# A two-layer diffusion backbone on one core: modulation in two half passes on VectorE, merges in PSUM, eight plain units at the start of each FFN

## The chip, the cores and the metric

One core of a Trainium2 chip. The metric is the device time of one execution in microseconds; of several runs the median counts.

## What is computed

Two layers over 640 tokens (128 context, 512 latent) of width 1024. Each layer, cut to what matters here:

```python
mod = silu(cond) @ w_mod + b_mod                  # 6 x 1024 per condition (context, latent)
sh1, sc1, g1, sh2, sc2, g2 = split(mod, 6)
h = rms_norm(x, norm1) * (1 + sc1) + sh1
u_f, q_g, k_g, v_g, r_g, a_g, q_d, k_d, v_d, gates = split(h @ w_in)
y_f = fourier_mix(u_f) @ w_fou
y_g = (rms_norm(gated_linear_attention(...)) * silu(r_g)) @ w_gla_o
y_d = rms_norm(differential_attention(...)) @ w_diff_o
gf, gg, gd = split(sigmoid(gates), 3)
merged = gf * y_f + gg * y_g + gd * y_d
x = x + g1 * (merged @ w_out)
h2 = rms_norm(x, norm2) * (1 + sc2) + sh2
x = x + g2 * ((silu(h2 @ w_ff_gate) * (h2 @ w_ff_up)) @ w_ff_down)
```

Outputs are x, and each layer's attention keys, values and linear-attention states of the context tokens.

## The kernel before

**Layout.** Activations lie channels by tokens: eight tiles of 128 x 640, worked on in two halves of 320 columns (`SPLIT`). A weight unit is 128 x 1024 floats, loaded as two 128 x 512 tiles by SP, and split into a high and a low part (`split_weight`, lines 436 to 460): ScalarE casts the high part (line 450), GpSimd subtracts to get the low one (line 454). A product is three matmuls, high x high, high x low, low x high (`acc3`, line 492). `group` accumulates one half's product of eight (or, in `merge`, four) blocks in a buffer `main` of PSUM, of which there are two; `misc` and `big` have two each.

**Order.** TensorE's order is the program's. In the mixer the other engines are ordered by the framework's scheduler, in which earlier instructions of the program go first when they are ready; around the output projection and the FFN their order is the program's too (`manual_schedule`). Every engine works its queue in order. After each group `slot(cols)` is called. It advances the side work of the mixer (`queue`: the Fourier mixing, the linear attention, the preparation of queries and keys, the attention), and counts columns towards `rate`: each time `rate` columns have gone by, the generator `self.back` makes one step. While the linear attention's levels run, `hold` sets the count to zero. `finish_back` makes all steps that are left, at once.

**Modulation.** The 48 tiles of `mod` (128 channels each, two conditions) come in two ways.
- On TensorE: `mod_load` brings 32 tiles of `w_mod`, `mod_first` multiplies them with the conditions (line 734), ScalarE copies the rows (line 740), a transpose and VectorE's adds (line 746) give `mod`. This serves tiles 0 to 15: of layer one at the start of the kernel, and of layer two through `mod_later` as `back` in layer one's FFN, at a rate of 1600 columns.
- On VectorE: `mod_next` loads the condition in four pieces (two conditions, two halves of the 1024 rows), applies silu, then loads the transposed weights (two halves of a tile) and sums products along the row (line 781), two instructions for a half of a tile. It runs for layer one's tiles 16 to 35 from the start of its mixer (rate 160) and 36 to 47 from the last branch's gates on (128); for layer two's 16 to 31 as `fill` between layer one's down-projections, and 32 to 47 from the gates of its last branch on (256).

**Branches.** A mixer projects and folds the Fourier input, then the linear attention's inputs, then those of the differential attention, one half of the heads at a time, with the Fourier branch's gates and merges between them and the linear-attention branch's after them; then the gates and the merges of the last branch, then the output projection. `merge` (line 1419) multiplies a branch by its output weights: ScalarE copies the product from PSUM to a tile `y` (line 1426), VectorE multiplies by the gate (lines 1428, 1430) and adds (line 1431); in the last branch the sum is split at once (lines 485, 486).

**FFN.** Four quarters of gate and up pairs, each followed by its down-projection. The first `AHEAD` = 6 weight units (three pairs) are plain: `first_four` begins four of them while the normalization is still under way (line 518), and `ffn_start` goes through the evictions (`gate`, lines 292 and 293; `up`, 297 and 298; `low`, 302), with `combine` (lines 859 to 885) between them, which forms the sums of activation blocks that the other pairs need. The other pairs are done in seven products of half the size each in place of eight (`gated`, line 562); their weights need sums, which VectorE forms in PSUM (lines 422 to 436) and splits (line 454). `last_sums` (line 887) splits four tiles more.

The lines that the change and the prediction's steps touch:

Of the kernel before, what the change touches and what calls it, by code (L numbers as in the profile page):

```python
# [12 lines left out]
F32 = mybir.dt.float32  # L13
# [4 lines left out]
ALU = mybir.AluOpType  # L18
# [241 lines left out]
def layout(i):  # L260
# [8 lines left out]
        "w_mod": np.concatenate([pack_mod(i["w_mod"][l]) for l in range(DEPTH)]),  # L269
        "w_modt": np.concatenate([pack_modt(i["w_mod"][l])[32:] for l in range(DEPTH)]),  # L270
# [34 lines left out]
class Kernel:  # L305
# [400 lines left out]
    def mod_load(self, c, l=0, ks=range(KT)):  # L706
        raws = []
        for k in ks:
            raws.append(self.unit("rawm")[:, :512])
            self.nc.sync.dma_start(raws[-1], self.a["w_mod"][(l * 4 + c) * KT + k])  # L710
        return raws

    def mod_later(self, l, small, mod, scale1):

        for c in range(4):
            raws = []
            first = self.mod_first(raws, c, small, mod, scale1)
            for ks in (range(4), range(4, KT)):
                raws += self.mod_load(c, l, ks)
                yield  # L720
                for _ in ks:
                    next(first, None)
                yield
            for _ in first:
                pass
# [26 lines left out]
    def mod_next(self, l, m0, m1, small, mod):  # L752

        nc = self.nc
        cond = {}
        for i in range(2):
            for k in range(2):
                cond[i, k] = self.unit("cond")[:, :512]
                nc.sync.dma_start(cond[i, k], self.a["cond_b"][:, i, k * 512 : (k + 1) * 512])
        yield  # L760
        ends = collections.deque()
        for i, k in [(i, k) for i in range(2) for k in range(2)] + [(None, None)]:
            if i is not None:
                ends.append(self.silu(cond[i, k], self.unit("cond_t")[:, :512]))
            if i is None or len(ends) > 1:
                ends.popleft()()
            yield
        todo = [(m, k) for m in range(m0, m1) for k in range(2)]
        raws = collections.deque()
        for n in range(len(todo) + 2):  # L770
            if n < len(todo):
                m, k = todo[n]
                raws.append(self.unit("rawm")[:, :512])
                nc.sync.dma_start(raws[-1], self.a["w_modt"][l * 64 + m * 2 + k - 32])
            if n >= 2:
                m, k = todo[n - 2]
                raw = raws.popleft()
                if k == 0:
                    sums = self.sm([P, 2, 2], "modsum", 3)
                for i in range(2):  # L780
                    nc.vector.scalar_tensor_tensor(  # L781
                        self.sm([P, 512], "junk", 1, mybir.dt.bfloat16), raw, 1.0, cond[i, k], op0=ALU.mult, op1=ALU.mult, accum_out=sums[:, i, k : k + 1]
                    )
                if k:
                    nc.vector.scalar_tensor_tensor(mod[:, m], sums[:, :, 0], small[:, S_BM + m : S_BM + m + 1], sums[:, :, 1], op0=ALU.add, op1=ALU.add)
            yield

# [692 lines left out]
    def mixer(self, l, h, small, backs, norms):  # L1480
        nc = self.nc

        if backs[0] is not None:
            self.back, self.rate = backs[0], 160
# [386 lines left out]
```

## Time and profile before

| | us |
|---|---|
| median of three runs | 2354.91 (2353.22 to 2359.13) |
| the profiled execution | 2363.46 |
| its span, first to last instruction | 2361.7 |
| TensorE busy | 2232.1 |
| VectorE busy | 1645.7 |
| ScalarE busy | 995.8 |
| GpSimd busy | 935.5 |

The profile names engines PE (TensorE; PEld its weight loads), DVE (VectorE), ACT (ScalarE), POOL (GpSimd) and SP (DMA issue). A stretch is a piece of the span. [...]

### The profile page before, as it was taken

Reading aid. Unit: us, or ns where it says so; the run is one execution under the profiler, and the core shown is the slowest. Engines: PE = TensorE matmul, PEld = TensorE weight load, DVE = VectorE, ACT = ScalarE, POOL = GpSimd, SP = SyncE. Lnnn points to the kernel's source line nnn. Section 1 sums busy time; section 2 is a strip of 40 time slices with the busy share of each in tenths; the row PEclk is TensorE's granted clock in tenths of the full one; section 3 lists DMA queues with packets and bytes.
Section 4 is the critical chain, followed back from the end, with each engine's and each line's share of the span. In section 5 each row is a group of like instructions: output and inputs, shape, how many; then the busy total and the mean of one; then the engine's idle time right before and its main releaser. Section 6 shows DMA issues by size and latency. Waiting matters only on the chain. (4 is left out here: it accounts for less than half of the span.)

```text
span 2361.7 us, 44422 instructions
## 1 busy us (share of the span) xinstructions
PE 2232.1 (95%) x16882; PEld 2183.9 (92%) x16882; DVE 1645.7 (70%) x3410; ACT 995.8 (42%) x2194; POOL 935.5 (40%) x771
## 2 busy tenths in 40 slices
PE   6989899999999899998989999999998998999999
PEld 4978899999899899998989999999998888999999
DVE  5797887685955857778764757857758667575674
ACT  3444446454234424241434554464633254242332
POOL 1342444352333634342433443535333255252433
PEclk9999999999999899999999999999999999999999
DMA  7443221112622272736242222212134322424433
GB/s 271 159 135 98 78 74 55 63 55 83 212 88 78 84 246 87 266 119 212 87 149 72 79 78 72 70 50 65 53 116 166 132 88 74 160 98 160 135 103 125
DMA packets 151382, 271.40 MB, mean 115 GB/s; under 512 B 19200, under 2 KB 31360, under 8 KB 151168
## 3 DMA queue, kind: packets, MB, share of 16 engines
q1 hardware_dynamic: 125824, 219.75, 28.6%
q10 hardware_dynamic: 25344, 48.80, 5.9%
q8 instruction: 133, 2.18, 0.4%
q14 instruction: 81, 0.66, 0.1%
HBM read 235.98 MB, written 27.79 MB: 112 GB/s over the span
## 5 line engine op out<-in xcount | busy, mean ns | idle before, releaser
L454 POOL TENSOR_TENSOR wl<-raw,wh 128x512 fp32r<-128x512 f32 x514 | 710.3, 1396 | 1105.6 <-ACT wh L450 956.9
L450 ACT CAST wh<-raw 128x512 fp32r<-128x512 f32 x518 | 314.8, 619 | 293.8 <-PE main L492 155.7
L492 PE MATMUL main<-hh,wh 128*128 128x320 f32 x936 | 294.8, 315 | 0.1
L492 PE MATMUL main<-hh,wl 128*128 128x320 f32 x936 | 289.6, 309 | 0.0
L492 PE MATMUL main<-hl,wh 128*128 128x320 f32 x936 | 289.5, 309 | 0.0
L781 DVE SCALAR_TENSOR_TENSOR junk<-rawm,cond 128x512 bf16<-128x512 f32 x256 | 225.5, 881 | 30.8 <-DMA rawm<-in_w_modt_dram 25.8
L492 PE MATMUL main<-wh,hh 128*128 128x256 f32 x800 | 234.6, 293 | 10.5 <-DVE rx L1472 5.3
L492 PE MATMUL main<-wl,hh 128*128 128x256 f32 x800 | 228.7, 286 | 0.0
L492 PE MATMUL main<-wh,hl 128*128 128x256 f32 x800 | 228.5, 286 | 0.0
L492 PE MATMUL main<-ah,wh 128*128 128x320 f32 x704 | 219.8, 312 | 6.9 <-DVE x L1453 5.6
L1453 DVE SCALAR_TENSOR_TENSOR x<-main,g,x 128x128 f32<-128x128 f32 (+2 forms) x240 | 97.3, 436 | 184.5 <-PE main L492 170.1
L492 PE MATMUL main<-ah,wl 128*128 128x320 f32 x704 | 217.5, 309 | 0.0
L492 PE MATMUL main<-al,wh 128*128 128x320 f32 x704 | 217.5, 309 | 0.0
L450 ACT CAST wh<-big 128x512 fp32r<-128x512 f32 x152 | 89.2, 587 | 261.4 <-DVE big L433 88.4
L492 PEld LDWEIGHTS main<-hh,wh 128*128 128x128 f32 x936 | 176.4, 189 | 0.9 <-DVE aT L1526 0.3
L492 PE MATMUL main<-h2h,wh 128*128 128x320 f32 x520 | 165.1, 318 | 12.4 <-DVE tt L297 6.4
L492 PEld LDWEIGHTS main<-hl,wh 128*128 128x128 f32 x936 | 176.3, 188 | 0.1
L492 PEld LDWEIGHTS main<-hh,wl 128*128 128x128 f32 x936 | 176.0, 188 | 0.0
L492 PEld LDWEIGHTS main<-wh,hh 128*128 128x128 f32 x800 | 155.9, 195 | 13.6 <-ACT tm L644 6.0
L492 PE MATMUL main<-h2l,wh 128*128 128x320 f32 x520 | 164.2, 316 | 0.0
L492 PE MATMUL main<-h2h,wl 128*128 128x320 f32 x520 | 164.0, 315 | 0.0
L492 PEld LDWEIGHTS main<-wl,hh 128*128 128x128 f32 x800 | 155.9, 195 | 0.0
(359 smaller groups left out, 6118.2 us busy)
## 6 DMA issues: line engine op xcount, KB each, us to landing
raw<-in_w_dram SPq DMA_DIRECT2D x556, 256.0 KB, 2.9
rawm<-in_w_modt_dram SPq DMA_DIRECT2D x128, 256.0 KB, 4.4
x<-xd ACTq DMA_DIRECT2D x64, 320.0 KB, 4.5
rawm<-in_w_mod_dram SPq DMA_DIRECT2D x64, 256.0 KB, 5.3
xd<-x ACTq DMA_DIRECT2D x48, 320.0 KB, 4.0
xd<-x ACTq DMA_DIRECT2D x48, 160.0 KB, 1.9
cond<-in_cond_b_dram SPq DMA_DIRECT2D x16, 256.0 KB, 4.6
x<-in_x_t_dram SPq DMA_DIRECT2D x12, 320.0 KB, 5.4
```

The source lines that it names most:

```text
L450: nc.scalar.copy(h, raw)
L454: (nc.vector if late or sums else nc.gpsimd).tensor_sub(lo, raw, h.bitcast(F32))
L492: mm = lambda w, x, first=False, last=False: nc.tensor.matmul(ps, w, x, start=first and not more, stop=last, skip_group_check=more)
L781: nc.vector.scalar_tensor_tensor(self.sm([P, 512], "junk", 1, mybir.dt.bfloat16), raw, 1.0, cond[i, k], op0=ALU.mult, op1=ALU.mult, accum_ ...
L1453: nc.vector.scalar_tensor_tensor(x[:, r], ps[:, r.start - s.start : r.stop - s.start], g[:, m, i : i + 1], x[:, r], op0=ALU.mult, op1=ALU.add)
```

## The change

- **Modulation.** `mod_later` and the part of `w_mod` for layer two go. `mod_next` makes two passes, one for each half of the 1024 rows, with two pieces of the condition each; the first pass leaves its sums in `mod`, the second adds its own and the bias. A weight tile is loaded one step ahead in place of two. Layer two's tiles 0 to 15 are the `fill` of layer one's FFN; each layer's tiles 16 to 47 run in its own mixer, from its start, at one step per 400 columns, and per 560 from the differential attention's inputs on, up to the `finish_back` at the mixer's end. `scale1` is then made by `mod_scale`, when the last tile of layer one's FFN is done.
- **Merge.** No copy to `y`: VectorE multiplies out of PSUM (first branch), or within it, and adds from there.
- **FFN.** `AHEAD` is 8: four pairs are plain in each layer. `up` of the fourth unit and the weights that follow the third go before `combine`'s second step; `low` comes one eviction later; `last_sums` is made in two parts, behind the first and the second product.
- `UNITS`, the number of 128 x 640 tiles in SBUF, is 59 in place of 58.

```diff
-UNITS = 58
-AHEAD = 6
+UNITS = 59
+AHEAD = 8
+MODT = (-32, 64)
+RATES = (400, 560)
...
     def mod_next(self, l, m0, m1, small, mod):
+        nc = self.nc
+        for k in range(2):
+            cond = [self.unit("cond")[:, :512] for _ in range(2)]
+            for i in range(2):
+                nc.sync.dma_start(cond[i], self.a["cond_b"][:, i, k * 512 : (k + 1) * 512])
             yield
+            end = self.silu(cond[0], self.unit("cond_t")[:, :512])
+            yield
+            end()
+            end = self.silu(cond[1], self.unit("cond_t")[:, :512])
+            yield
+            end()
+            raw = None
+            for m in range(m0, m1 + 1):
+                last, raw = raw, None
+                if m < m1:
+                    raw = self.unit("rawm")[:, :512]
+                    nc.sync.dma_start(raw, self.a["w_modt"][MODT[l] + 2 * m + k])
+                if last is not None:
+                    sums = mod[:, m - 1] if k == 0 else self.sm([P, 2], "modsum", 3)
+                    for i in range(2):
+                        nc.vector.scalar_tensor_tensor(
+                            self.sm([P, 512], "junk", 1, mybir.dt.bfloat16), last, 1.0, cond[i], op0=ALU.mult, op1=ALU.mult, accum_out=sums[:, i : i + 1]
+                        )
+                    if k:
+                        b = small[:, S_BM + m - 1 : S_BM + m]
+                        nc.vector.scalar_tensor_tensor(mod[:, m - 1], sums, b, mod[:, m - 1], op0=ALU.add, op1=ALU.add)
+                yield
...
-    def last_sums(self, xs, act):
-        for k in range(4):
+    def last_sums(self, xs, act, ks):
+        for k in ks:
             self.split(xs[k][:, SPLIT[1]], *act["T3"][k])
...
             ps = self.group(self.weight(l, u), (m % 2) * 4, 4, act, s)
-            y = self.unit("y")[:, s]
-            nc.scalar.copy(y, ps)
             if first:
-                nc.vector.scalar_tensor_tensor(merged[m][:, s], tg[:, s], 1.0, y, op0=ALU.add, op1=ALU.mult)
+                nc.vector.scalar_tensor_tensor(merged[m][:, s], tg[:, s], 1.0, ps, op0=ALU.add, op1=ALU.mult)
             else:
-                nc.vector.scalar_tensor_tensor(tg[:, s], tg[:, s], 1.0, y, op0=ALU.add, op1=ALU.mult)
-                nc.vector.tensor_add(merged[m][:, s], merged[m][:, s], tg[:, s])
+                nc.vector.scalar_tensor_tensor(ps, tg[:, s], 1.0, ps, op0=ALU.add, op1=ALU.mult)
+                nc.vector.tensor_add(merged[m][:, s], ps, merged[m][:, s])
...
+        self.back, self.rate = back, RATES[0]
...
         dact = []
+        self.rate = RATES[1]
         for pr in range(2):
...
-        self.finish_back()
-        self.back, self.rate = backs[1], 128 if l == 0 else 256
         tg = [self.gate(l, U_BR[2] + m, h) for m in range(KT)]
...
         self.group_to(last, self.weight(l, us[3]), h2, SPLIT[1])
+        acts[1].up(last, 1)
+        self.used(l, us[2])
         next(combine)
         acts[0].low(1)
-        acts[1].up(last, 1)
-        self.used(l, us[2])
         for i in range(4, AHEAD):
             for p in range(2):
                 ps = self.group(self.weight(l, us[i]), 0, KT, h2, SPLIT[p])
                 if i % 2 == 0:
                     acts[i // 2].gate(ps, p)
-                    next(combine, None)
                 else:
                     acts[i // 2].up(ps, p)
-                if i == 4:
-                    acts[1].low(1) if p == 0 else self.used(l, us[3])
-                elif p:
-                    self.used(l, us[4])
-                    self.used(l, us[5])
-        for p in range(2):
-            acts[2].low(p)
+                if p:
+                    self.used(l, us[3 if i == 4 else i])
+                    if i == 5:
+                        self.used(l, us[4])
+                next(combine, None)
+                if i % 2 or p == 0:
+                    acts[(i - 1) // 2].low(p if i % 2 else 1)
...
-                self.last_sums(x2, sums)
-                if back is not None:
-                    self.back, self.rate = back, 1600
+                for i in range(2):
+                    self.after(i + 1, lambda i=i: self.last_sums(x2, sums, range(2 * i, 2 * i + 2)))
...
-            mg, x2 = self.mixer(l, h, small, (None, later_mod(32, 48)) if l else (later_mod(16, 36), later_mod(36, 48)), norms)
+            mg, x2 = self.mixer(l, h, small, self.mod_next(l, 16, 48, small, mod), norms)
...
+                    scales.append(self.mod_scale(n_mod, n_small, S_N1, 8, "scale1"))
...
-                    l, h2, x2, combine, sums, first, g2, done, self.mod_later(l + 1, n_small, n_mod, scale1), self.mod_next(l + 1, 16, 32, n_small, n_mod)
+                self.ffn(l, h2, x2, combine, sums, first, g2, done, self.mod_next(l + 1, 0, 16, n_small, n_mod))
```

## Rows read from the trace of the kernel before

**Rows 1.** The page: the span; part 1 for TensorE (busy us, share, instructions)

```profile
span 2361.7 us, 44422 instructions
...
PE 2232.1 (95%) x16882; PEld 2183.9 (92%) x16882; DVE 1645.7 (70%) x3410; ACT 995.8 (42%) x2194; POOL 935.5 (40%) x771
```

**Rows 2.** Stretches: length, busy us (count) of PE, PEld, DVE, ACT, POOL; clock, DMA

```profile
71.40:304.60 233.20, 209.37 (x2085) 202.13 (x2083) 195.25 (x410) 103.12 (x224) 85.49 (x65) 0.96 0.36 114
1256.00:1465.30 209.30, 203.04 (x2084) 196.99 (x2083) 125.68 (x227) 103.95 (x224) 79.16 (x65) 0.99 0.26 77
304.60:632.90 328.30, 323.45 (x2357) 321.61 (x2356) 245.37 (x585) 160.37 (x403) 136.65 (x126) 1.00 0.27 87
1465.30:1793.60 328.30, 323.46 (x2357) 321.62 (x2356) 233.18 (x552) 160.37 (x403) 136.56 (x126) 1.00 0.24 77
632.90:672.10 39.20, 32.36 (x194) 30.78 (x193) 32.43 (x64) 16.05 (x38) 11.40 (x9) 0.91 0.31 101
1793.60:1835.90 42.30, 31.39 (x194) 29.73 (x193) 36.71 (x82) 15.86 (x37) 12.47 (x9) 0.96 0.46 156
672.10:733.20 61.10, 58.46 (x396) 57.65 (x395) 26.54 (x62) 19.30 (x43) 18.18 (x15) 1.00 0.31 100
1835.90:1902.30 66.40, 60.99 (x397) 59.79 (x396) 43.91 (x113) 19.54 (x43) 19.09 (x15) 0.95 0.39 133
733.20:803.10 69.90, 59.32 (x348) 57.70 (x346) 49.73 (x85) 33.71 (x75) 39.87 (x33) 0.88 0.19 63
1902.30:1973.40 71.10, 60.73 (x347) 59.09 (x346) 49.72 (x85) 33.65 (x74) 39.83 (x33) 0.86 0.19 62
803.10:1179.40 376.30, 364.57 (x2624) 358.02 (x2625) 277.83 (x534) 133.95 (x249) 150.70 (x108) 0.99 0.50 167
1973.40:2322.60 349.20, 348.09 (x2364) 346.81 (x2365) 221.10 (x369) 130.86 (x241) 149.41 (x108) 1.00 0.39 128
```

**Rows 3.** Stretches, line 734 alone: length, PE and PEld busy, clock, DMA, GB/s

```profile
800.00:1000.00 200.00, 6.48 (x192) 4.88 (x192) 0.99 0.55 184
1000.00:1100.00 100.00, 2.16 (x64) 1.62 (x64) 1.00 0.51 170
```

**Rows 4.** TensorE in time, layer one's opening: start, us, what [idle before <-releaser]

```profile
736.46 0.41 PE L518 MATMUL big<-h2h,wh 128*128 128x320 f32 x1 [1.75 <-ACT wh L450]
...
737.99 0.41 PE L518 MATMUL big<-h2h,wl 128*128 128x320 f32 x1 [0.97 <-POOL wl L454]
...
779.30 0.41 PE L492 MATMUL main<-h2h,wh 128*128 128x320 f32 x1 [2.64 <-DVE tt L293]
...
791.33 0.61 PE L492 MATMUL main<-h2h,wh 128*128 128x320 f32 x1 [3.19 <-DVE tt L297]
...
803.10 0.42 PE L492 MATMUL misc<-h2h,wh 128*128 128x320 f32 x1 [1.91 <-DVE e L598]
```

**Rows 5.** TensorE in time: last merges of both layers, and line 746's pause

```profile
644.38 0.64 PE L492 MATMUL main<-dh,wh 128*128 128x320 f32 x1 [4.83 <-ACT y L1426]
...
1082.70 0.39 PE L492 MATMUL main<-ah,wh 128*128 128x320 f32 x1 [1.31 <-DVE mod L746]
...
1810.27 0.42 PE L492 MATMUL main<-dh,wh 128*128 128x320 f32 x1 [4.61 <-ACT y L1426]
...
1843.36 0.64 PE L492 MATMUL main<-mh,wh 128*128 128x320 f32 x1 [4.05 <-ACT mh L485]
```

**Rows 6.** Three lines' instructions: count, ns min/median/max, first and last start, shape

```profile
L1428 DVE SCALAR_TENSOR_TENSOR mg<-tg,y x32: 478/485/1591, 308.1 to 1564.8; 128x320 f32<-128x320 f32 x32
...
L598 DVE TENSOR_TENSOR e<-misc,e x38: 475/482/492, 802.6 to 2315.8; 128x320 f32<-128x320 f32 x38
...
L1426 ACT COPY y<-main x96: 414/423/444, 306.6 to 1838.7; 128x320 f32<-128x320 f32 x96
```

**Rows 7.** VectorE's groups by form: count | busy us, mean ns | idle before

```profile
L781 DVE SCALAR_TENSOR_TENSOR junk<-rawm,cond 128x512 bf16<-128x512 f32 x256 | 225.5, 881 | 30.8 <-DMA rawm<-in_w_modt_dram 25.8
```

**Rows 8.** Stretch of layer two's first query and key preparation, columns as Rows 2

```profile
1465.00:1515.00 50.00, 49.94 (x349) 49.44 (x348) 43.69 (x108) 22.08 (x49) 22.55 (x22) 1.00 0.23 71
```

More of the change, by code (lines that the diff above doesn't have):

```diff
@@ L268, in layout @@
         "cond_b": np.broadcast_to(cond.T.reshape(1, 2, D), (P, 2, D)),
-        "w_mod": np.concatenate([pack_mod(i["w_mod"][l]) for l in range(DEPTH)]),
-        "w_modt": np.concatenate([pack_modt(i["w_mod"][l])[32:] for l in range(DEPTH)]),
+        "w_mod": pack_mod(i["w_mod"][0]),
+        "w_modt": np.concatenate([pack_modt(i["w_mod"][l])[0 if l else 32 :] for l in range(DEPTH)]),
         "small": np.stack([pack_small(i, l) for l in range(DEPTH)]),
@@ L703, in load_small, with mod_load @@
         return s, mod
-    def mod_load(self, c, l=0, ks=range(KT)):
+    def mod_load(self, c):
         raws = []
-        for k in ks:
+        for k in range(KT):
             raws.append(self.unit("rawm")[:, :512])
-            self.nc.sync.dma_start(raws[-1], self.a["w_mod"][(l * 4 + c) * KT + k])
+            self.nc.sync.dma_start(raws[-1], self.a["w_mod"][c * KT + k])
         return raws
[L713 to L725, printed above, removed]
     def mod_first(self, raws, c, small, mod, scale1):
@@ L754, in mod_next @@
         nc = self.nc
[L755 to L766, printed above, removed]
-            yield
@@ L768, in mod_next @@
[L768 to L785, printed above, removed]
-            yield
+        for k in range(2):
+            cond = [self.unit("cond")[:, :512] for _ in range(2)]
+            for i in range(2):
+                nc.sync.dma_start(cond[i], self.a["cond_b"][:, i, k * 512 : (k + 1) * 512])
+            yield
+            end = self.silu(cond[0], self.unit("cond_t")[:, :512])
+            yield
+            end()
[18 more added lines that the diff above has]
+                yield
@@ L1478, in rgate, with mixer @@
                 )
-    def mixer(self, l, h, small, backs, norms):
+    def mixer(self, l, h, small, back, norms):
         nc = self.nc
-        if backs[0] is not None:
-            self.back, self.rate = backs[0], 160
+        self.back, self.rate = back, RATES[0]
         tab = {}
@@ L1627, in ffn_start, with ffn @@
         return {f: a.out for f, a in enumerate(acts)}
-    def ffn(self, l, h2, x2, combine, sums, norms, g2, done, back=None, fill=None):
+    def ffn(self, l, h2, x2, combine, sums, norms, g2, done, fill=None):
         nc = self.nc
@@ L1813, in run @@
             n_small, n_mod = later[l]
-            scale1 = self.lp.tile([P, KT, 2], F32, tag="scale1", name=self.name("scale1"), bufs=2)
             n_acc = self.unit("acc")
-            first, keep, norms = norms, [], []
+            first, keep, scales, norms = norms, [], [], []
             def done(xs, m, s):
@@ L1821, in done @@
                 if m == KT - 1 and s.start == 0:
[L1822 removed]
+                    scales.append(self.mod_scale(n_mod, n_small, S_N1, 8, "scale1"))
                     keep.append(self.pairs("h", KT))
[L1824 removed]
+                norm_steps(m, int(s.start > 0), lambda p: self.modulate(xs, n_acc, scales[0], n_mod, 0, p, keep[0]), -3, None, 0, 1)
             with self.tc.manual_schedule(engines=FFN_ORDERED):
[L1827 to L1829 removed]
+                self.ffn(l, h2, x2, combine, sums, first, g2, done, self.mod_next(l + 1, 0, 16, n_small, n_mod))
             h = keep[0]
```

5 lines of the change are left out of this document (removed).

## The prediction

> **What bounds the kernel now.** The profiled execution took 2363.5 us, 2361.7 of it the span [rows 1]; the median of the runs is 2354.9, 0.36% less, and what I add up against the first I take off the second. TensorE is busy 95% of the span [rows 1], so time can come only from three places: fewer matmuls, fewer pauses of TensorE, and less of its half-speed time after pauses. I read the stages against each other, because the two layers issue the same matmuls with different side work. Six stretches are cut at the first matmul of a kind: front (line 1524 to the first merge), middle (to the last branch's merges), merges (to the output projection), projection (to the FFN), opening (to the fifth product of the first seven-product pair), rest (to the last quarter's down-projection). For each, [rows 2] has layer one and then layer two, with the matmuls in brackets. Undisturbed work is the last row: 349.2 us for 2364 matmuls at full clock, 0.148 us each. The reader is to see:
> - front: 233.2 us in layer one, 209.3 in layer two, for the same matmuls. Layer one runs its modulation sums there (VectorE 195 us against 126), layer two runs none.
> - middle: 328.3 us in both, to the tenth. VectorE is at 75% and 71% and costs nothing.
> - merges plus projection: 100.3 and 108.7 us, where 590 matmuls are worth 87.3.
> - opening: 69.9 and 71.1 us where 348 matmuls are worth 51.5, at a clock of 0.88 and 0.86: paused, then half speed.
> - rest: 376.3 in layer one against 349.2; layer one has 260 more matmuls and more VectorE work there.
>
> **A, modulation off TensorE (layer one's FFN).** `mod_later` goes: 256 matmul records in the FFN, 6.48 + 2.16 = 8.6 us of TensorE [rows 3], all on the path since TensorE is the bound; two records stand for one matmul. With it go eight switches into and out of that shape, and a pause of 1.3 us on the transposed result (line 746) [rows 5]. I put the switches at 0.2 us each, an estimate, so 1.6. Its 32 loads on SP's queue go, but the row sums of other tiles keep their number in this FFN (64 of them before and after), so nothing else moves. Sum -11.5, between -8.6 (nothing but the matmuls) and -16 (some of the remaining 15 us that separate the two rest stretches was its work too). The two tail steps of the sums, drained before the last quarter, now hold a load; I count that inside the bound.
>
> **B, eight plain units open the FFN.** One pair leaves the seven-product form: 96 matmuls in place of 84, +12 x 0.148 = 1.8 us per layer. In return the pauses of the opening [rows 4]: 2.64 us (a gate's eviction behind the sums that prepare pair weights, line 293), 3.19 (an `up` eviction behind `combine` and the same sums, line 297) and 1.91 (line 598, behind `last_sums`). After the change the units whose weights are prepared at that point are plain, so ScalarE and GpSimd prepare them and VectorE has no pair sums until `combine` is over; `up` of unit 3 goes ahead of `combine`; `last_sums` waits for a product or two. The first two pauses, 1.75 and 0.97 on the first weights, are untouched, with a loss to the half clock behind them that I put at 3.4 us, two fifths of the 0.12 x 69.9 = 8.4 us that the clock costs here. Removable: 69.9 - 51.5 - 2.7 - 3.4 = 12.3 us, and I use it for both layers. VectorE has 50 us of work in an opening of 70 [rows 2]; it keeps nearly that, in some 14 us more. I take 9 of the 12.3, since `combine` itself still runs among the first evictions. Sum 2 x (1.8 - 9) = -14.4, between +3.6 (the pauses only move) and -21.
>
> **C, merges and projection.** ScalarE's copy, 96 x 0.42 us (line 1426) [rows 6], goes; VectorE reads PSUM, writes the product back there, and adds from there. TensorE's two-buffer `main` is then free after two VectorE instructions, not one copy. What one costs: with a PSUM operand 0.482 us median and 0.492 at most (line 598); with both in SBUF 0.485 median, but up to 1.59 (line 1428), when GpSimd is at work [rows 6]. So 160 instructions keep their median and lose their tail. [...]
> The pauses here were 4.83 us in layer one, where 24 tiles' sums at one step per 128 columns had VectorE behind when the merges began, and 4.61 and 4.05 among six in layer two, where sums ran through the merges [rows 5]. Counting `slot` calls in the mixer (holds of the linear attention skipped), the new rates issue four steps in the 16 merges of either layer, where layer one had none and layer two ten, and leave ten of 72 steps undone in layer one and six in layer two; `finish_back` drains them in one go, where nine were drained in layer two before. A step is two sums of 0.88 us [rows 7]. What is queued behind the drained sums on VectorE is the projection's `residual`, and TensorE's third group waits for that; in layer two nine drained steps cost the projection 66.4 against 61.1. The merges want 16 x 3 x 0.49 = 23.5 us of VectorE plus 4 x 1.8, in 28.7 us of matmuls: close to the bound, so 33 us, not 28.7. With 61 for the projection and 1 for the drain: 95 in both layers. Sum -5 and -14, -19; between -8 (VectorE stays the bound) and -25 (both at their matmuls' pace).
>
> **D, layer one's front.** 48 steps at one per 160 columns become 17 at one per 400 until the second hold ends. The cost of the sums was 233.2 - 209.3 = 23.9 us. In proportion 17/48 leaves 8.5; with no queue behind VectorE it leaves nothing. I take 6, nearer to the proportion: -18, between -15 and -24.
>
> **E, layer two's front.** The same load where none was: +6, between 0 and +8.5. Seven more steps, of 21 by its end, fall before it, among the normalization of the first four units, where VectorE is in TensorE's chain: +2, between 0 and +4.5. Sum +8.
>
> **F, the middle.** 41 steps per layer in place of 32 and 20. At 1.8 us a step VectorE gets some 20 and 42 us more, less 7 for merges without tails: 258 and 268 of 328 us, 79% and 82%. Layer one's front lost its 24 us at 84%, so there is room, but little where query and key preparation runs: there it has 43.7 of 50 us already [rows 8], and five steps make it 52. I take +4 for both layers, between 0 and +30.
>
> **G, PSUM held through VectorE.** In the first two branches a gate's group follows the second half's merge, and needs the buffer of the first half's. TensorE gets there after 12 x 0.148 = 1.8 us; two VectorE instructions are 1.0, and whatever is queued ahead of them adds. Before, a ScalarE copy of 0.42 us had this place, and TensorE was busy 323.5 of the middle's 328.3 us [rows 2]. There are 32 such places, a few of them late: +4, between -2 and +15.
>
> **The sum.** -11.5 - 14.4 - 19 - 18 + 8 + 4 + 4 = -47 us: 2316 in the profiled execution's terms, 2308 in the median's. I say 2310.
>
> **Rivals.**
> - VectorE becomes the bound of the middle (slower). Place: query and key preparation and the softmax steps, twice per layer, where TensorE's transposes wait for VectorE in order. It decides once a stretch wants more of VectorE than its matmuls last; [rows 8] plus five steps says just over. If the middle then loses what layer one's front lost, 24 of 233 us, that is 34 per layer, 68 in all for the 4 counted: 2374. For it: the 52 in 50. Against: 79 to 82% on the mean, and no loss at 87% there today. Chance 0.06.
> - The opening's pauses only move, and late merges cost their bound: B +4 and G +15, 30 us worse: 2339. For it: `combine` stays where it is. Against: what was late there was queued behind pair sums that are no longer there. Chance 0.17.
> - The sums are not spread as it says: the ten drained steps meet the loads of `x2` and of the weights on SP's queue, VectorE waits in order for a tile, and C gives only -8, D -15: 14 us worse, 2324. Chance 0.17.
> - More comes back: without pauses the clock stays up in the fronts and openings: B -21, C -25, D -24, some 19 us better: 2291. Chance 0.12.
>
> **How the numbers follow.** The forecast has a chance of 0.48; its own range is 2296 to 2330. The range of 8 in 10 reaches from a little past the better case to a little past the second rival: 2284 to 2346. A measurement of this kernel tells 0.3%, 7 us, from no change. Faster than that: the forecast, the better case, the third rival and most of the second, 0.86; within: the rest of the second and a mild form of the first, 0.08; slower: 0.06.
>
> **What would show it.** Line 734 only in the first 60 us; no line 1426; 320 sums in place of 256; TensorE's pauses at lines 293, 297 and 598 gone from the opening. In stretches: fronts near 215 us both, middles near 332, merges plus projection near 95, openings near 75 with 96 more matmuls at a clock over 0.93, rests near 352 and 337. It is wrong if a middle is over 340, if merges that read PSUM take over 0.6 us on the mean, or if an opening keeps pauses over 2 us behind VectorE.

## The result and the profile after

The changed kernel takes 2380.19 us (median of four, 2375.77 to 2388.88) against 2355.52 (2353.22 to 2359.13): a ratio of 1.0108, with a 95% interval of 1.0074 to 1.0142. It is slower by 25 us, where I forecast 47 us faster. The profiled execution is the slowest of the four, 2388.88 us; its span is 25.4 us longer than the one of before [rows 1].

The page of the changed kernel: the span, and part 1 for TensorE.

```profile
span 2387.1 us, 43828 instructions
...
PE 2238.0 (94%) x16646; PEld 2185.1 (92%) x16646; DVE 1648.7 (69%) x3512; ACT 954.2 (40%) x2084; POOL 940.0 (39%) x777
```

TensorE has 236 matmul records fewer and is busy 6 us longer; it is idle for 149.1 us of the span in place of 129.6. Its granted clock, where 1.00 is full speed, is 0.979 over either span, but 0.98 and 0.99 in the middles, which were at 1.00. Its stretches, cut and laid out as [rows 2] (front, middle, merges, projection, opening, rest; layer one, then layer two):

```profile
70.20:285.10 214.90, 204.50 (x2083) 198.24 (x2082) 145.62 (x283) 103.72 (x224) 80.08 (x65) 0.98 0.31 92
285.10:641.50 356.40, 334.29 (x2357) 328.48 (x2356) 259.81 (x655) 147.57 (x369) 137.63 (x126) 0.98 0.28 88
641.50:677.50 36.00, 30.78 (x194) 29.73 (x193) 29.13 (x65) 11.65 (x24) 11.16 (x9) 0.95 0.43 146
677.50:737.80 60.30, 58.46 (x397) 57.66 (x395) 42.26 (x112) 18.56 (x41) 19.81 (x15) 1.00 0.42 141
737.80:817.50 79.70, 71.24 (x444) 69.08 (x442) 53.73 (x89) 37.55 (x82) 48.05 (x40) 0.94 0.20 62
817.50:1178.80 361.30, 340.71 (x2280) 336.03 (x2281) 269.42 (x505) 126.43 (x234) 146.13 (x104) 1.00 0.45 149
1256.80:1482.70 225.90, 210.88 (x2084) 204.33 (x2083) 146.95 (x292) 104.08 (x226) 81.98 (x66) 0.95 0.30 90
1482.70:1831.50 348.80, 329.91 (x2357) 324.67 (x2356) 260.93 (x661) 147.76 (x369) 137.69 (x126) 0.99 0.28 90
1831.50:1868.90 37.40, 31.47 (x195) 30.68 (x194) 27.64 (x65) 11.70 (x24) 11.19 (x9) 0.91 0.42 139
1868.90:1929.20 60.30, 58.45 (x396) 57.65 (x396) 35.19 (x91) 18.55 (x41) 18.92 (x15) 1.00 0.37 124
1929.20:2008.90 79.70, 71.18 (x444) 69.08 (x443) 53.71 (x89) 37.58 (x82) 47.84 (x40) 0.94 0.20 62
2008.90:2347.80 338.90, 337.51 (x2281) 335.97 (x2282) 210.68 (x354) 124.67 (x230) 143.68 (x104) 0.99 0.40 131
```

Against [rows 2]: fronts -18.3 and +16.6, middles +28.1 and +20.5, merges with projections -4.0 and -11.0, and opening with rest and what follows to the next layer -3.8 and -1.5. Most of what is lost lies in the middles: +48.6. VectorE is busy 73 and 75% of them, with no more work than I had worked out (258 and 268 us forecast, 260 and 261 measured).

**Where in the middle.** I cut each where TensorE first transposes the queries of the second pair of heads (line 1317 of before). The first part holds nearly all of the query and key preparation, the Fourier branch's gates and merges, the first attention, and the first two of the sixteen half merges of the linear-attention branch; call it the branches' part. The second holds the other fourteen, the second attention and the last branch's gates; call it the last branch's part. The sums (line 781 of before, 766 of after) alone, per part of both layers; columns: length, VectorE busy in these sums, records (two for a sum), clock, DMA. Before:

```profile
304.60:480.10 175.50, 0.00 (x0) 1.00 0.19 63
480.10:632.90 152.80, 37.97 (x79) 1.00 0.36 115
...
1465.30:1640.80 175.50, 0.00 (x0) 1.00 0.20 63
1640.80:1793.60 152.80, 26.13 (x51) 1.00 0.28 94
```

After:

```profile
285.10:485.70 200.60, 30.20 (x72) 0.96 0.26 81
485.70:641.50 155.80, 36.62 (x73) 1.00 0.29 96
...
1482.70:1677.10 194.40, 25.27 (x60) 0.98 0.25 81
1677.10:1831.50 154.40, 42.01 (x87) 1.00 0.31 100
```

The kernel before ran no sum at all in the branches' part, and 40 and 26 in the last branch's, where they cost nothing: both parts last the same in both layers to the tenth. All of these lie under the last branch's gates, which end the part. Layer one's last part before, cut behind the linear-attention branch's last merge (all instructions, columns as in [rows 2]):

```profile
480.10:576.40 96.30, 94.74 (x684) 94.11 (x683) 67.51 (x157) 53.18 (x137) 40.10 (x35) 1.00 0.17 55
576.40:632.90 56.50, 56.50 (x387) 56.50 (x386) 47.80 (x101) 18.33 (x36) 22.27 (x16) 1.00 0.67 218
```

Under the gates VectorE is busy 85% of the time and TensorE never pauses (56.50 of 56.50 us busy). ScalarE takes the gates out of PSUM, so TensorE waits for nothing of VectorE there.

The change puts 36 and 30 sums into the branches' part, where there were none, and there 25.1 and 18.9 us go, 44 of the 48.6. How full VectorE is there was to be seen before the change, had I cut finer. The branches' part of layer one in four pieces, all instructions, columns as in [rows 2]; before, then after:

```profile
304.60:330.70 26.10, 26.06 (x182) 25.78 (x181) 24.45 (x64) 10.35 (x20) 11.64 (x12) 1.00 0.19 60
330.70:354.20 23.50, 23.48 (x166) 23.25 (x165) 18.87 (x45) 11.71 (x28) 10.61 (x10) 1.00 0.25 82
354.20:455.70 101.50, 99.80 (x781) 99.31 (x780) 66.02 (x171) 54.52 (x151) 38.39 (x39) 1.00 0.17 55
455.70:480.10 24.40, 22.87 (x167) 22.65 (x166) 20.72 (x54) 12.28 (x31) 13.63 (x15) 1.00 0.25 79
```

```profile
285.10:312.70 27.60, 26.54 (x181) 25.77 (x180) 25.57 (x69) 8.51 (x15) 11.30 (x12) 1.00 0.25 75
312.70:340.80 28.10, 25.41 (x167) 24.89 (x166) 23.90 (x60) 10.19 (x24) 11.95 (x12) 0.94 0.30 95
340.80:450.90 110.10, 103.45 (x782) 101.50 (x780) 76.42 (x211) 51.83 (x144) 37.54 (x38) 0.97 0.25 78
450.90:485.70 34.80, 26.50 (x167) 25.75 (x166) 28.09 (x77) 11.48 (x29) 16.82 (x19) 0.90 0.27 85
```

VectorE was at 94, 80, 65 and 85% of the four pieces before; the three full ones hold most of the preparations. Of the 25.1 us that the four lose together, TensorE is busy 9.7 longer, at a granted clock down to 0.90 where it was 1.00, and idle for the rest. Behind the first of the pauses shown next the clock is 0.57 (346 to 352 us), behind the second 0.76 (459 to 466). TensorE in time, after: three of its pauses in this part (start, us, what [idle before <-releaser]).

```profile
346.52 0.64 PE L496 MATMUL main<-hh,wh 128*128 128x320 f32 x1 [5.35 <-DVE mg L1412]
...
460.06 1.02 PE L1268 MATMUL big<-const,y 128*128 128x128 f32 x5 [5.01 <-DVE kT L1224]
...
477.01 0.42 PE L496 MATMUL main<-hh,wh 128*128 128x320 f32 x1 [2.39 <-DVE mg L1415]
```

And what stood ahead of the second of them in VectorE's queue, after:

```profile
454.13 0.68 DVE L766 SCALAR_TENSOR_TENSOR junk<-rawm,cond 128x512 bf16<-128x512 f32 x1
...
455.08 0.68 DVE L766 SCALAR_TENSOR_TENSOR junk<-rawm,cond 128x512 bf16<-128x512 f32 x1
...
455.80 0.76 DVE L766 SCALAR_TENSOR_TENSOR junk<-rawm,cond 128x512 bf16<-128x512 f32 x1
...
456.60 1.63 DVE L766 SCALAR_TENSOR_TENSOR junk<-rawm,cond 128x512 bf16<-128x512 f32 x1
458.16 0.08 DVE L766 DVE_READ_ACCUMULATOR junk<-rawm,cond 128x1 f32 x1
458.27 0.29 DVE L1224 TENSOR_TENSOR kx<-big,kx 64x128 fp32r<-64x128 f32 x1
...
459.22 0.69 DVE L1224 TENSOR_TENSOR kT<-big,kT 64x512 fp32r<-64x512 f32 x1 [0.45 <-ACT kT L1223]
```

Four sums, two steps of the generator, run from 454.13 to 458.24 with one short product of the preparation (0.42 us) among them; none of them waited for its tile. The key's evictions that TensorE waits for come right behind them. Before, this pause was 1.53 us:

```profile
461.36 0.74 PE L1282 MATMUL big<-const,y 128*128 128x128 f32 x5 [1.53 <-DVE kT L1238]
```

Three theories: **V**, VectorE's queue works in order, and sums put into the branches' part delay what TensorE needs, whatever the mean load; **L**, the sums themselves are late, since the tile is asked for one step ahead in place of two: the idle time of the sums' group is 123.8 us after, 120.1 of it on the tile's load, where it was 30.8 [rows 7]; **M**, the merge in PSUM holds TensorE's buffer through two instructions of VectorE.

```profile
L766 DVE SCALAR_TENSOR_TENSOR junk<-rawm,cond 128x512 bf16<-128x512 f32 x320 | 287.1, 897 | 123.8 <-DMA rawm<-in_w_modt_dram 120.1
```

### The profile page after: what moved, and what is told of

It is laid out like the page before. It is cut to its first block, busy times and chain, and to the rows that moved or that the text cites. A ratio compares the mean times of both kernels' runs of the same rounds, so it can differ in the third digit from the quotient of the medians.

```text
span 2387.1 us, 43828 instructions
## 1 busy us (share of the span) xinstructions
PE 2238.0 (94%) x16646; PEld 2185.1 (92%) x16646; DVE 1648.7 (69%) x3512; ACT 954.2 (40%) x2084; POOL 940.0 (39%) x777
## 3 DMA queue, kind: packets, MB, share of 16 engines
q1 hardware_dynamic: 125248, 218.70, 28.7%
## 5 line engine op out<-in xcount | busy, mean ns | idle before, releaser
L766 DVE SCALAR_TENSOR_TENSOR junk<-rawm,cond 128x512 bf16<-128x512 f32 x320 | 287.1, 897 | 123.8 <-DMA rawm<-in_w_modt_dram 120.1
L496 PE MATMUL main<-hh,wh 128*128 128x320 f32 x936 | 301.1, 322 | 28.9 <-DVE mg L1412 17.7
L496 PE MATMUL main<-hl,wh 128*128 128x320 f32 x936 | 294.3, 314 | 0.0
L454 ACT CAST wh<-big 128x512 fp32r<-128x512 f32 x144 | 84.4, 586 | 258.1 <-DVE big L437 86.8
L496 PE MATMUL main<-h2h,wh 128*128 128x320 f32 x560 | 176.3, 315 | 8.6 <-DVE tt L297 6.4
L496 PE MATMUL main<-h2l,wh 128*128 128x320 f32 x560 | 175.2, 313 | 0.0
L496 PE MATMUL main<-h2h,wl 128*128 128x320 f32 x560 | 174.9, 312 | 0.0
```

Of the source, the lines that this page charges most:

```text
L454: nc.scalar.copy(h, raw)
L496: mm = lambda w, x, first=False, last=False: nc.tensor.matmul(ps, w, x, start=first and not more, stop=last, skip_group_check=more)
L766: nc.vector.scalar_tensor_tensor(self.sm([P, 512], "junk", 1, mybir.dt.bfloat16), last, 1.0, cond[i], op0=ALU.mult, op1=ALU.mult, accum_ou ...
```

## The experiments

Ratios are against the kernel before on the same chip, with 95% intervals. Stretches are from each kernel's trace; "branches" is the branches' part, "last" the last branch's, "FFN" runs from the first product of the FFN to the next front, in layer two to its last quarter's down-projection. The names of the two middle parts are those from above.

| us | ratio | front 1 | branches | last | merges | proj. | FFN | front 2 | branches | last | merges | proj. | FFN |
|---|---|---|---|---|---|---|---|---|---|---|---|---|---|
| before | 1 | 233.2 | 175.5 | 152.8 | 39.2 | 61.1 | 522.8 | 209.3 | 175.5 | 152.8 | 42.3 | 66.4 | 420.3 |
| the change | 1.0108 | 214.9 | 200.6 | 155.8 | 36.0 | 60.3 | 519.0 | 225.9 | 194.4 | 154.4 | 37.4 | 60.3 | 418.6 |
| merge alone | 1.0017 | 231.8 | 183.5 | 152.4 | 36.7 | 59.3 | 521.8 | 208.0 | 184.5 | 152.4 | 39.9 | 60.6 | 415.3 |
| modulation alone | 1.0183 | 216.3 | 199.4 | 161.7 | 35.5 | 62.2 | 516.7 | 222.8 | 195.4 | 162.6 | 35.3 | 63.7 | 418.5 |
| eight units alone | 0.9981 | 233.0 | 175.5 | 152.8 | 37.1 | 61.1 | 514.2 | 208.9 | 177.0 | 152.8 | 41.7 | 66.4 | 417.7 |
| change, two ahead | 1.0059 | 217.7 | 197.0 | 158.3 | 34.4 | 60.9 | 504.8 | 222.6 | 192.2 | 160.2 | 36.2 | 60.3 | 414.3 |
| change, sums without loads | 1.0081 | 218.9 | 183.5 | 174.0 | 28.7 | 59.3 | 502.2 | 225.0 | 187.8 | 173.1 | 28.8 | 59.2 | 412.5 |
| change, loads without sums | 0.9829 | 212.3 | 191.6 | 152.8 | 30.2 | 60.2 | 496.4 | 215.6 | 188.2 | 152.6 | 32.0 | 59.3 | 414.7 |
| change, sums held | 1.0042 | 213.9 | 177.2 | 153.9 | 61.1 | 59.3 | 507.2 | 222.9 | 175.9 | 155.8 | 54.6 | 59.2 | 414.9 |
| two ahead, PSUM last | 1.0072 | 215.7 | 197.0 | 160.5 | 36.0 | 61.0 | 504.1 | 226.3 | 189.8 | 163.2 | 35.7 | 60.3 | 415.7 |
| before, eight, PSUM last | 0.9907 | 232.2 | 175.4 | 152.9 | 37.1 | 59.3 | 512.8 | 209.3 | 175.6 | 152.8 | 39.9 | 60.5 | 414.8 |
| the same, sums moved | 0.9967 | 225.9 | 176.6 | 152.9 | 47.0 | 59.3 | 521.4 | 207.9 | 175.4 | 152.9 | 46.5 | 59.2 | 413.6 |

The branches' part is the same within 1.5 us in every kernel that leaves it alone; the FFN of layer one is not that steady. A trace is one execution and lies up to 13 us from its kernel's median.

### The parts one by one

Merge alone: the kernel before with the changed lines of `merge`, nothing else.

```diff
-            y = self.unit("y")[:, s]
-            nc.scalar.copy(y, ps)
             if first:
-                nc.vector.scalar_tensor_tensor(merged[m][:, s], tg[:, s], 1.0, y, op0=ALU.add, op1=ALU.mult)
+                nc.vector.scalar_tensor_tensor(merged[m][:, s], tg[:, s], 1.0, ps, op0=ALU.add, op1=ALU.mult)
             else:
-                nc.vector.scalar_tensor_tensor(tg[:, s], tg[:, s], 1.0, y, op0=ALU.add, op1=ALU.mult)
-                nc.vector.tensor_add(merged[m][:, s], merged[m][:, s], tg[:, s])
+                nc.vector.scalar_tensor_tensor(ps, tg[:, s], 1.0, ps, op0=ALU.add, op1=ALU.mult)
+                nc.vector.tensor_add(merged[m][:, s], ps, merged[m][:, s])
```

> The kernel before with the merge in PSUM alone (no ScalarE copy; modulation and FFN opening as before). Theory M (TensorE pays for a PSUM buffer that is freed by two instructions of VectorE, whenever VectorE is late): the middles grow by 15 us or more each, and what the merges give back (8 to 10 us in all) does not cover it: 2360 to 2385. Theories L (the sums wait for a weight tile that is loaded one step ahead) and V (the sums are simply too much work for VectorE in the middle): the middles stay within 3 us of 328, the merges gain: about 2346.

2361.85 us, 1.0017 (1.0004 to 1.0031): 4 us slower. The branches' parts grow by 8.0 and 9.0 us without one sum in them, the merges and projections give back 4.3 and 8.2. M holds, at a little over half the loss that I expected of it. Nearly all of it lies between the first and the last merge of the Fourier branch (7.1 and 7.9 us), in the middle of the preparations. The last branch's parts, with fourteen of the sixteen half merges of the linear-attention branch, lose nothing (152.4 against 152.8).

Modulation alone: the changed kernel with `merge`, `AHEAD`, `UNITS`, `ffn_start` and `last_sums` of before.

> The changed kernel with the merge by ScalarE's copy and the FFN opening with six plain units: only the modulation is changed. Theories L and V: middles at 345 to 360 us, layer one's front near 215, layer two's near 226, so some 2370 to 2390, as slow as the whole change or slower. Theory M: middles near 332 and a time near 2345, faster than before.

2402.96 us, 1.0183 (1.0160 to 1.0205): 43 us slower, more than the whole change. The branches' parts take 199.4 and 195.4 us with ScalarE's copy, as long as with the merge in PSUM, and the last branch's parts 161.7 and 162.6, longer than with it. The modulation is the loss.

Eight units alone: the kernel before with the FFN part.

```diff
-AHEAD = 6
+AHEAD = 8
...
-                self.last_sums(x2, sums)
+                for i in range(2):
+                    self.after(i + 1, lambda i=i: self.last_sums(x2, sums, range(2 * i, 2 * i + 2)))
```

> The kernel before with eight plain units opening each FFN alone. All theories: the two openings take 79 to 80 us with 96 more matmuls (14.2 us of matmuls moved there from the rest), net 4 to 5 us a layer, so about 2345. If part B was worth the 14 us forecast and other parts of the change eat it, 2341 or less; if the pauses only move, 2353 to 2358.

2353.02 us, 0.9981 (0.9967 to 0.9996): 4.5 us faster by the medians, at the edge of the case in which the pauses only move; in the traces the two FFNs give 8.6 and 2.6 us. Either way B is worth less than the 14.4.

### Waiting or working

Two ahead: the changed kernel, its loads one step earlier.

```diff
-            raw = None
-            for m in range(m0, m1 + 1):
-                last, raw = raw, None
-                if m < m1:
...
+            raws = collections.deque()
+            for n in range(m0, m1 + 2):
+                if n < m1:
+                    raws.append(self.unit("rawm")[:, :512])
+                    nc.sync.dma_start(raws[-1], self.a["w_modt"][MODT[l] + 2 * n + k])
+                if n >= m0 + 2:
+                    m = n - 1
+                    last = raws.popleft()
```

> The changed kernel, but each sum's weight tile is asked for two steps before it is used, as the kernel before does, in place of one. Theory L: VectorE's idle time on the tile falls from 124 us to under 40, the middles go to 330 to 338 and layer two's front under 218: about 2335. Theories V and M: the idle time falls too, but the middles stay above 345: 2365 to 2380.

2370.52 us, 1.0059 (1.0038 to 1.0081): 10 us faster than the change. Layer one's FFN takes 504.8 us in place of 519.0 (507.2 and 504.1 in the two later kernels with the tile two ahead); the middles stay. The idle time of the sums' group hardly falls, from 123.8 to 111.0, and it matters where it falls. In layer one's FFN VectorE's idle time on the tile goes from 11.9 to 1.6 us, and TensorE's pauses behind the residual's add go with it. What waited for what there (us, times, longest), the change, then two ahead:

```profile
PE main L496 <- DVE x L1437: 18.1, 19, 2.0
...
PE main L496 <- DVE x L1438: 6.7, 9, 1.7
```

In the branches' part of layer one it stays as it was:

```profile
DVE junk L766 <- DMA rawm<-in_w_modt_dram: 7.5, 3, 4.1
...
DVE junk L767 <- DMA rawm<-in_w_modt_dram: 7.7, 3, 4.1
```

So this run shows what the late tile costs the FFN. Of L in the middle it is no test, since the wait there did not change (in layer two 3.2 us, then 3.6). But these waits are small beside the 25.1 and 18.9 us that the two parts lost, and the pause of 5 us behind the four sums is there again (5.03), with no wait for a tile ahead of it. In the last branch's parts VectorE stands 26.4 and 24.9 us for the tile under the change, and they grow by 3.0 and 1.6.

Sums without loads: `raw = cond[0]` in place of the tile and its load.

> The changed kernel, its sums reading a tile that is already in SBUF in place of the weights, so that no sum waits for a load and SP's queue carries 320 tiles' halves fewer; VectorE's work is the same (its sums are those of another tile). Theory V (VectorE's own work, in order ahead of the query and key preparation and the merges, holds TensorE): from the first merge to the last branch's start the layers stay near 200 and 194 us and layer two's front near 226; only the FFN of layer one gains, as with the tile asked for two steps ahead (14 us): about 2365. Theory L (the wait for the tile): these stretches go back to 184 us and layer two's front to 212: about 2335.

2377.23 us, 1.0081 (1.0066 to 1.0096); the profiled execution, 2364.34, is the fastest of nine. This run did not do what it was meant to: with nothing to wait for, the scheduler drew the sums together, 64 into layer one's front and 64 into its last branch. So it says nothing of L in the branches' part, which held none in layer one and took the 183.5 us of the merge alone. It shows what sums do that wait for no tile. The last branch's part takes 174.0 us in place of 152.8, and 57 of its 64 sums lie ahead of the gates, among the linear-attention branch's merges, where the kernel before has none. That piece takes 112.8 us, against 96.0 with the merge alone, and VectorE is busy 97% of it:

```profile
472.60:585.40 112.80, 99.24 (x684) 95.86 (x683) 109.03 (x299) 49.59 (x126) 39.31 (x34) 0.98 0.14 46
```

Loads without sums: a small copy in place of both sums.

```diff
-                    for i in range(2):
-                        nc.vector.scalar_tensor_tensor(
-                            self.sm([P, 512], "junk", 1, mybir.dt.bfloat16), last, 1.0, cond[i], op0=ALU.mult, op1=ALU.mult, accum_out=sums[:, i : i + 1]
-                        )
+                    nc.vector.tensor_copy(sums, last[:, :2])
```

> The changed kernel with the same loads of the weights at the same steps, but a copy of two elements of each tile in place of its two sums over 512: the wait stays, VectorE's work goes (the modulation is left out by it). Theory V: the stretch from the first merge to the last branch's start falls to 184 us in both layers (175.5 before plus the 8 to 9 that the merge in PSUM alone costs there), layer two's front to 210 to 213, layer one's front to 210, the rest of layer one's FFN by 15 or more: about 2315. Theory L: the wait stays in front of the same instructions: no stretch gains over 5 us, and 2365 to 2380.

2318.60 us (two runs), 0.9829 (0.9807 to 0.9852), 62 us faster than the change: as V has it for the whole. In the branches' part it is both. Without the sums the layers take 191.6 and 188.2 us, 8.1 and 3.7 above the merge alone; the sums' work adds 9.0 and 6.2. The 8.1 and 3.7 are not the wait alone: VectorE stands 5.9 and 1.5 us for the tile there, and has 3.7 and 4.8 us more work than with the merge alone (the conditions' silu, the small copies). Here is the wait, in VectorE's queue of this run, what ScalarE makes of it, and TensorE's pause that follows:

```profile
453.75 0.77 DVE L1221 TENSOR_TENSOR kT<-kc,kT 64x128 fp32r<-64x128 f32 x1
458.63 0.17 DVE L765 COPY mod<-rawm 128x2 f32<-128x2 f32 x1 [4.11 <-DMA rawm<-in_w_modt_dram]
458.71 0.28 DVE L1221 TENSOR_TENSOR kT<-kc,kT 64x128 fp32r<-64x128 f32 x1
...
459.33 0.58 ACT L1220 CAST kT<-big 128x512 fp32r<-128x512 f32 x1 [4.68 <-DVE kx L1221]
...
462.60 0.63 PE L496 MATMUL main<-oh,wh 128*128 128x320 f32 x1 [2.96 <-ACT tg L1400]
```

VectorE stands 4.11 us for a tile with a key's eviction behind it; ScalarE waits for that, and its gate for TensorE is late. My expectation of 184 us by V was 4 to 8 us too low, and L has a share.

### Place

Before, eight, PSUM last: the kernel before with eight units, and the merge in PSUM where `parts` is given, in the last branch.

> The kernel before with two parts of the change: eight plain units open each FFN, and the merge in PSUM in the last branch alone (the first two branches keep ScalarE's copy). By theories M and V the 8 to 9 us that the merge in PSUM costs from the first merge to the last branch's start do not arise, its gain after that (12 us in the merges and projections of both layers, some 5 in the openings) stays, and eight units give 4.5: 2336 to 2345, faster than before. If the gain at the end is only loss carried over from the first branches, 2350 to 2356.

2336.70 us, 0.9907 (0.9889 to 0.9924): faster than both kernels, by 22 us on the same chip's runs of before. The merge in PSUM gains in the last branch, and the copy kept in the first two saves what it cost there, which by the merge alone is the Fourier branch's part. It was not tried in the linear-attention branch and the last together.

Sums held:

```diff
-RATES = (400, 560)
+RATES = (300, 1 << 30, 96)
...
+        self.rate, self.due = RATES[2], 0
         tg = [self.gate(l, U_BR[2] + m, h) for m in range(KT)]
```

> The changed kernel with the tile asked for two steps ahead, the merge in PSUM in the last branch alone, and the sums held from the first branch's merges to the last branch's gates, where the kernel before has none; to make up, one step per 300 columns ahead of that (23 to 37 steps by then) and one per 96 after. Theory V: the stretch from the first merge to the last branch's start falls from 200 and 194 to 176 us in both layers; the last branch's stretch takes 155 to 160, where 152.8 held 20 steps at no cost; layer one's front 218, layer two's 226; FFN one like the run two steps ahead: about 2330. If the sums cost TensorE the same wherever they lie, the last branch's stretch grows by what the other gives and the time is 2355 to 2365.

2368.56 us, 1.0042 (1.0028 to 1.0057): no better than two ahead. The branches' parts go back to 177.2 and 175.9, as V says, and the last branch's parts hold 49 sums, all under the gates, at 1 to 3 us; but 46 and 36 sums are left for the merges, which take 61.1 and 54.6 us. My arithmetic of what one step per 96 columns would get through was wrong. What is taken out of one full place has to find another, and the merges have none (VectorE is busy 56.88 of their 61.10 us in layer one):

```profile
616.30:677.40 61.10, 33.88 (x192) 32.06 (x193) 56.88 (x162) 11.83 (x25) 13.01 (x9) 0.80 0.34 108
```

Two ahead, PSUM last: two ahead with that `merge`.

> The changed kernel with the tile asked for two steps ahead and the merge in PSUM in the last branch alone, the sums left where the change puts them. If the loss of the merge in PSUM and that of the sums add up (each holds TensorE by itself), the stretch from the first merge to the last branch's start falls from 196 and 194 us by the 8 to 9 that the merge in PSUM costs alone, to 187 and 185, and the time from 2370 to some 2353. If both are the same lateness of VectorE's queue, seen at two places, the stretch stays at 192 or more, as it did with the sums spread and the copy kept in all branches (199), and the time at 2362 to 2370.

2375.53 us, 1.0072 (1.0047 to 1.0098): 197.0 and 189.8 us in the branches' parts, and a time above both my cases. The two losses don't add up; with the sums there, the queue is as late with the copy as without.

The same, sums moved: "before, eight, PSUM last" with 64 of layer one's sums in its front and 64 from the gates on, both layers at 128 columns.

```diff
-(later_mod(16, 36), later_mod(36, 48))
+(later_mod(16, 32), later_mod(32, 48))
...
-        self.back, self.rate = backs[1], 128 if l == 0 else 256
+        self.back, self.rate = backs[1], 128
```

> The kernel before with eight plain units, the merge in PSUM in the last branch alone, and its own modulation moved a little by place: layer one runs 64 sums instead of 80 in its front and 64 instead of 48 from the last branch's gates on, and layer two's 64 sums go at one step per 128 columns from there instead of 256, so that 40 lie in the last branch's stretch, where the kernel before has 40 at no cost. Theory V (a sum costs by the place where it lies): layer one's front 5 us less (0.3 us a sum), its projection 1 us more, layer two's merges 3 us less: 2325 to 2332. If the place does not matter, 2334 to 2340.

2348.82 us, 0.9967 (0.9951 to 0.9983): 12 us slower than without it, and above both my cases. The front gained 6.3 us, but in the merges, where 8 and 19 sums had run, there are now 24 and 22, and they take 9.9 and 6.6 us more. In layer two it can't be the number, which hardly rose; it is the order. There the sums had been spread over the merges, one or two to a merge; now they stand one behind another ahead of the first merge's add, in both layers, and TensorE pauses for all of them at once. TensorE's idle time in layer one's merges, and the one pause in layer two's:

```profile
L492 PE MATMUL main<-dh,wh 128*128 128x320 f32 x64 | 20.9, 326 | 16.5 <-DVE mg L1427 16.5
...
1810.34 0.63 PE L492 MATMUL main<-dh,wh 128*128 128x320 f32 x1 [16.69 <-DVE mg L1427]
```

Another 8.6 us went in layer one's FFN, where nothing differs. TensorE is idle there hardly longer than without the move (27.5 us, 26.4), but busy 493.9 us in place of 486.5, at a mean granted clock of 0.97 in place of 0.99; what lowered it isn't known.

## Why the prediction was wrong

The forecast was -47 us in the profiled execution's terms, the trace says +25.4, 72 us apart: some 41 of them in the middles, 20 in the FFNs, 9 in layer two's front and 4 in the merges and projections. By the prediction's steps:

- **F and G, the middle: the step that failed.** +8 forecast, +48.6 measured. F took the middle as one stretch, found VectorE at 75 and 71% there with 32 and 20 steps that cost nothing, and put +4 on 9 and 21 more. But the sums that cost nothing all lay under the last branch's gates, where TensorE waits for nothing of VectorE, and those of the change are spread over the whole middle. By itself, with ScalarE's copy kept, F cost 62.5 us (modulation alone: middles of 361.1 and 358.0 us against 328.3), twice its bound of 30; with the merge in PSUM on top the middles are 13.9 us shorter, so F and G can't be added, and why it is shorter wasn't tested. I had taken a value at the foot of the bound because the mean was low. Rival one named place, mechanism and price: the preparation of queries and keys, TensorE waiting for VectorE in order, 34 us per layer. It got 28.1 and 20.5, and 32.8 and 29.7 with the modulation alone. I gave it 0.06, for "79 to 82% on the mean" and "no loss at 87% there today". The mean hid a piece of 26.1 us at 94%. The 87% is [rows 8], 43.69 of 50: that very place, and without one sum in it, so it said nothing of what sums would do there and should have set the value.
- **G** was mis-sized by itself too: +4 for both layers, against +8.0 and +9.0 with the merge alone, 17.0 together and past its bound of 15. Its working said that "whatever is queued ahead of them adds", and then took only a few of the 32 places as late. The late ones are the Fourier branch's, among the preparations. The instructions cost what I said: line 1412 478 ns, 1414 489, 1415 483 at the median, none over 497. The tail of line 1428 before, which they were to lose, went with GpSimd: all 8 of the 32 that took over 520 ns, up to 1591, overlap an instruction of GpSimd. Those that read PSUM show none: 30 of line 598's 38 lie under one, and the longest takes 492.

- **E, layer two's front.** +6 forecast for the front itself, +16.6 measured, past its bound of 8.5; the piece ahead of it, where I put +2, grew by 1.4. With the loads but no sums the front is 215.6 us, so 6.3 of the 16.6 are there without the sums, and their work is 10.3. I had counted the work alone, in layer one's proportion. Layer one's front, with 28 sums against 30 and as long a wait for the tile (20.4 us against 21.4), is 5.6 us above the 209.3; why layer two's pays three times that isn't known.
- **A and B, the FFN.** -25.9 forecast, -5.5 in the trace. Asked for two steps ahead, the FFNs give -18.0 and -6.0, -24 together. Part of the difference is the tile asked for late, which the diff shows and I did not price. But 4.3 us of it lie in layer two's FFN, which holds no sum, and by the medians the earlier tile is worth 9.7, not 18.5; the change's trace lies 8.7 above its median. So A and B together gave between some 14 (5.5 and 8.7) and 24, an estimate from these numbers, under the forecast. How it divides into A and B isn't measured. The eight switches of shape, 0.2 us each in A, are in the trace of before: on the way into line 734 a matmul starts 0.24 us after the one ahead of it, on the way out 0.25, where 0.15 is usual (from 832.75 and from 834.00), 0.2 us more in all. By medians B alone is worth 4.5 us; its trace reads 11, so one of the two flatters. The first two pauses of [rows 4] are there still (1.7 and 1.0 us), and the other three are 5.2 us together in place of 7.7. TensorE in layer one's opening, after:

```profile
781.97 0.41 PE L496 MATMUL main<-h2h,wh 128*128 128x320 f32 x1 [0.73 <-DVE tt L297]
788.25 0.64 PE L496 MATMUL main<-h2h,wh 128*128 128x320 f32 x1 [2.48 <-DVE tt L297]
817.53 0.39 PE L496 MATMUL misc<-h2h,wh 128*128 128x320 f32 x1 [1.97 <-DVE e L602]
```

- **C, merges and projection.** -19 forecast, -15.0 measured, well inside its bounds; in "before, eight, PSUM last" it gives -12.2, without G's cost.
- **D, layer one's front.** -18 forecast, -18.3 measured.

What I said would prove me wrong did: a middle over 340 us (both are), and pauses over 2 us behind VectorE in an opening.

## What to carry to other kernels

- Before side work is moved, show where its instructions are now, stretch by stretch, how full the engine is in pieces as short as the chain that TensorE waits in (here 25 us, not 330), and whether TensorE waits for that engine there at all: under the last branch's gates VectorE was 85% busy at no cost, in the branches' part 74%, and sums put there cost most of their length (0.66 us of some 0.9). "It costs nothing today" holds for the place where it is today.
- VectorE, busy 74% of the branches' part and working in order, had no room where one of its short instructions stands between two matmuls: four sums ahead of a key's eviction went with a pause of 5.01 us, which was 1.53 before. And a wait at the head of its queue (a tile asked for late) cost as work does: 4.11 us of VectorE's, with 2.96 of TensorE's behind it.
- A copy that another engine makes to free a PSUM buffer was worth keeping where the reader's queue holds long work that TensorE needs (the Fourier branch's merges, among the preparations: without it the branches' parts took 8.0 and 9.0 us more), and worth dropping where TensorE waits on that reader's result anyway (4.3 and 8.2 us less in the merges and projections).

## What the runs showed that I had not expected

- One and the same sum of 0.9 us costs TensorE nothing, or most of its own length, by its place: 40 under the last branch's gates 0 us; 36 in the branches' part 23.9 with their waits (modulation alone), 0.66 each; 16 more in layer one's merges 9.9, 0.62 each.
- The losses behind this queue did not add: the merge in PSUM cost 17 us in the branches' parts by itself, and 1.2 and -1.0 on top of the modulation's sums (the change less modulation alone). In the last branch's parts it even takes 5.9 and 8.2 us off.
